# The first pair after a mixture's plain start: x and routing weights by TensorE, or by transposing DMAs and DRAM

## The chip, the cores and the metric

The kernel runs on one core of a Trainium2 chip. TensorE (PE in the profile) multiplies matrices into PSUM; VectorE (DVE), ScalarE (ACT) and GpSimd (POOL) work beside it, and SyncE (SP) issues DMAs, as ScalarE and GpSimd also do. Each engine runs its own list of instructions in order, and an instruction that waits holds all that stand behind it on its engine. The metric is the device time of one execution in microseconds; less is better.

## The reference

For 16 x 512 tokens of 512 features, a softmax over 8 experts gives each token eight routing weights. Every expert is applied to every token, and the results are added with these weights:

```python
probs = softmax(router_logits)                 # 16 x 512 x 8
for e in range(n_experts):                     # 8 experts
    expert_out = np.matmul(x, expert_weights[e])      # 512 x 2048 each
    output += probs[:, :, e:e+1] * expert_out
```

With the eight experts laid side by side this is one product. The left operand z has 8,192 rows of 8 x 512 numbers, x times the routing weight of each expert; the right operand is the 4,096 x 2,048 matrix of all weights.

## The kernel before, in words

**Products.** The product is cut by Strassen's method in Winograd's form, which takes seven products of halves in place of eight. The outer cut makes seven products P1 to P7 of (pairs of) blocks of 256 tokens, four experts and 1,024 columns. Sixteen pairs of token blocks are numbered q. Within one of the outer products the inner cut does the same with 128 tokens, two experts and 512 columns: seven *steps*, in the order 1, 5, 6, 2, 7, 3, 4 (`STEPS`), each of eight matmuls of 512 columns. A *stage* is two such products worked off in turn, step by step, and stages are run one after the other by `run`.

**Third cut.** In most stages steps 1 and 5 of both products are cut a third time (`by_thirds`, class `Thirds`): 14 small products of four matmuls of 256 columns stand in place of four steps of eight matmuls of 512. This needs four more operands from VectorE (operands 5, 6, 3 and 7, made from the z of both products) and small evictions: `ps<-pt,z` and `ps<-ps,z` of 256 columns on VectorE, copies on ScalarE. Before, this is done for stages 1 to 6 of the first outer product and not for stage 0.

**Left operands.** A `Left` holds the z of one product for two experts at a time (`make(0)`, `make(1)`), each one multiplication of a transposed x tile (xT, features by tokens) by a tile pT of routing weights that are the same on all 128 partitions. `queue_s2` makes the operand of step 6 (d), `queue_i` that of steps 7 and 3 (the row `z<-z,d`). The right operands of steps 5, 6, 7 and 4 are differences of the weight blocks (`inner_sums`, rows `w<-w`).

**Order.** VectorE's work waits in a queue of tasks written out by hand. `slack` takes tasks from it while a planned VectorE time (`clock["dve"]`) stays behind a planned TensorE time (`clock["pe"]`); `need` forces a task, with all ahead of it, when a step wants it. From `ordered[0] = True` on, program order is kept on each engine. In the start-up code before that, the framework's scheduler may set the instructions of an engine in another order than the text has.

**The start.** Pairs q = 0 and 1 of P1 are computed without Strassen's method, for two column halves n = 0 and 1, while weights arrive. Their z is made by TensorE: x times a diagonal matrix of routing weights (`early_z0`). GpSimd's queue casts x and weights from f32 to f16 on the way in: two x blocks, three weight blocks of two halves (512 KB in f16 each), then the x of q = 2 and 3 (`cast_x(4)`, `cast_x(6)`), the fourth weight block, and the x of stage 1. `softmax_of_all` computes all routing weights and SP stores them in DRAM (`p_dram`), from which later stages load them, spread over the partitions.

**Stage 0** is q = 2 and 3 of P1. Its xT and pT come from TensorE: `early_xp1`, called for two row blocks each after e = 0 and e = 1 of the plain part's n = 1, transposes x by matmuls with the identity (`ps<-ident,w`) and spreads the weights over the partitions by a matmul of ones with a diagonal (`ps<-h,ones`). VectorE and ScalarE copy the results to SBUF (lines 264 and 262). For that a second small softmax (`early_p(1)`) and four diagonals (`diag_j`) are made on VectorE from logits that SP loads on their own (`load_lg0(1)`).

The last four results of the plain part are copied by ScalarE (line 357) and stored by SP (`kept`).

Of the kernel before, what the change touches and what calls it, by code (L numbers as in the profile page):

```python
# [31 lines left out]
def kernel(  # L32
# [79 lines left out]
    def tt(o, a, b, op):  # L112
        dve(nc.vector.tensor_tensor(out=o, in0=a, in1=b, op=op))  # L113
# [9 lines left out]
    def sp(o, i):  # L123
        note(nc.sync.dma_start(out=o, in_=i))
# [94 lines left out]

    def load_lg0(t):  # L220
        rows = lg_f.rearrange("(q h) e -> q h e", h=2 * HQ)[ds(2 * t, 2), 0:HQ]
        tile_ = lg0[t].rearrange("p (q j) e -> p q j e", j=2)
        if t == 0:
            sp(tile_, rows.rearrange("q (p j) e -> p q j e", p=P))
        else:
            for q in range(2):
                sp(tile_[:, q], rows[q].rearrange("(j p) e -> p j e", p=P))
    lg0 = [cpool.tile([P, 4, E], f32, name=f"lg0_{t}") for t in range(2)]
    load_lg0(0)
    cast_x(0)  # L230
# [6 lines left out]
    with behind():  # L237
        for kn in BLOCKS[:3]:
            cast_block(11, kn, b11[kn], 2 if kn == (0, 0) else 1)
    cast_x(4)  # L240
    cast_x(6)
    cast_block(11, BLOCKS[3], b11[BLOCKS[3]])

    def early_p(t):
        if t == 0:
            return softmax(lg0[t], 4, cpool.tile([P, HE, 4], f16, name="ph0"))
        pf = softmax(lg0[t], 4, cpool.tile([P, HE, 4], f32, name="pf0"))
        odd = pf.rearrange("p e (q j) -> p e q j", j=2)[:, :, :, 1]
        tt(odd[:, 0:2], odd[:, 0:2], odd[:, 2:4], ADD)
        ph = cpool.tile([P, HE, 4], f16, name="ph1")  # L250
        dve(nc.vector.tensor_copy(ph, pf))
        return ph

# [11 lines left out]

    z0 = [zpool.tile([P, HE, C, P], f16, name="z", tag="z") for j in range(4)]
    ph0 = [early_p(0)]

    def diag_e(e):
        return diag(ph0[0][:, e].unsqueeze(2))  # L270

# [6 lines left out]

    ones = cpool.tile([P, P], f16, name="ones")
    nc.vector.memset(ones, 1.0)  # L280
    xp1 = [[xpool.tile([P, C, HQ], f16, name=name, tag="x") for name in ("xT", "pT")] for t in range(2)]

    def diag_j(j):
        return diag(ph0[1][:, :, ds(j % 4, 1)])

    def early_xp1(j, d):
        t, rows = j // 2 - 2, ds(j % 2 * P, P)
        ps = (bank, bank2)[j % 2]()
        for c in range(C):
            mm(ps[:, ds(c * P, P)], xs0[:, j, ds(c * P, P)], ident, c == 0, c == C - 1)  # L290
        evacuate(xp1[t][0][:, :, rows], ps.rearrange("p (c t) -> p c t", c=C), 0)
        ps = (bank, bank2)[j % 2]()
        mm(ps, ones, d.rearrange("p e t -> p (e t)"), True, True)
        evacuate(xp1[t][1][:, :, rows], ps.rearrange("p (e t) -> p e t", e=HE), 1)

# [6 lines left out]
    def load_logits():  # L302
        dve(nc.vector.memset(lg_all[:, 0, 0:1], 0.0))
        dve(nc.vector.memset(lg0[1][:, 0, 0:1], 0.0))
        load_lg0(1)
        for r in range(R):
            sp(lg_all[ds(r * NHQ, NHQ)], lg_v[r])

    def softmax_of_all():
# [11 lines left out]
        for r in range(R):  # L321
            sp(p_dram[:, :, ds(r * J, J)], ph[ds(r * NHQ, NHQ)])

    kept = [dram.tile([2, HQ, NB], f32, name=f"kept_{i}") for i in range(NI)]

# [5 lines left out]
    for n in range(2):  # L331
        ps = [bank2() if n == 0 and j < 2 else bank() for j in range(4)]
        for e in range(HE):
            if n == 0 and e < 2:
                early_z0(e + 2, ds_[e + 2])
                if e == 0:
                    ds_.append(diag_e(3))
            if n == 0 and e == 2:
                ph0.append(early_p(1))
                ds_ = [diag_j(j) for j in range(4, 8)]  # L340
                softmax_of_all()
                w, sums = inner_sums(b11, new_w())
                third = {1: third_sums(w[1])}
# [4 lines left out]
            if n == 1:  # L348
                for j in ((4, 5), (6, 7), (), ())[e]:
                    early_xp1(j, ds_[j - 4])  # L350
                if e == 0:
                    sums[5]()
                elif e == 1:
                    third[5] = third_sums(w[5])
        for j in range(4):
            o = half()
            act(nc.scalar.copy(o, ps[j]))
            sp(kept[j // 2][n].rearrange("(p j) m -> j p m", j=2)[j % 2], o)

    ordered[0] = True  # L360
# [4 lines left out]
    queue = deque()  # L365
    clock = {"pe": 0.0, "dve": 0.0}

# [433 lines left out]
    right = {r: Right() for r in (2, 5, 6, 7, 4, 3)}  # L801
    right[1] = Right(w, {p: Task(2.29, sums[p]) for p in (6, 7, 4)})
    lefts, xs, ps_, bases = {}, {}, {}, {}
# [779 lines left out]

    for stage in range(1, ND):
        thirds[stage] = Thirds(*(p.left for p in stages[stage]), third)
# [55 lines left out]
```

## Time and profile before

| what | us |
|---|---|
| median of 3 runs | 1351.97 (1351.48 to 1352.87) |
| the profiled execution | 1351.78 |
| its span, first to last instruction | 1350.1 |
| TensorE matmuls busy | 1344.0 |
| VectorE busy | 1166.9 |
| ScalarE busy | 281.9 |
| GpSimd busy | 403.9 |

The profiled execution is 1.7 us longer than its span and 0.2 us under the median. In the timeline a row has a start, a length, the engine, the line, the operation and `out<-in` with the program's names, `xN` for N instructions in a row, and in brackets the idle time before it and what ended it. DMA rows give the issuing queue, the size and the microseconds from issue to landing; rows of q0 and q1 give packets, MB and the packets' time as a share of the 16 engines' (it may exceed 100% where packets overlap). q0 carries GpSimd's casts, q1 SP's DMAs.

### The profile page before, as it was taken

Reading aid. Unit: us, or ns where it says so; the run is one execution under the profiler, and the core shown is the slowest. Engines: PE = TensorE matmul, PEld = TensorE weight load, DVE = VectorE, ACT = ScalarE, POOL = GpSimd, SP = SyncE. Lnnn points to the kernel's source line nnn. Section 1 sums busy time; section 2 is a strip of 40 time slices with the busy share of each in tenths; the row PEclk is TensorE's granted clock in tenths of the full one; section 3 lists DMA queues with packets and bytes.
Section 4 is the critical chain, followed back from the end, with each engine's and each line's share of the span. In section 5 each row is a group of like instructions: output and inputs, shape, how many; then the busy total and the mean of one; then the engine's idle time right before and its main releaser. Section 6 shows DMA issues by size and latency. Waiting matters only on the chain.

```text
span 1350.1 us, 19508 instructions
## 1 busy us (share of the span) xinstructions
PE 1344.0 (100%) x7122; PEld 694.3 (51%) x7122; DVE 1166.9 (86%) x1483; ACT 281.9 (21%) x593; POOL 403.9 (30%) x619
## 2 busy tenths in 40 slices
PE   9999999999999999999999999999999999999998
PEld 4465655565544444444444444554555455556564
DVE  7878898989989889797897889889898989898984
ACT  3342423223211111111111100110111111224331
POOL 3123322333323232323312112424334231232342
PEclk9999999999999999999999999999999999999999
DMA  9999989989899999999998889999999989999997
GB/s 181 242 222 240 239 264 242 291 284 290 247 329 282 323 288 286 295 306 265 318 325 265 295 313 189 243 239 216 244 249 226 219 219 310 308 178 230 262 163 132
DMA packets 185392, 346.26 MB, mean 256 GB/s; under 512 B 52176, under 2 KB 81616, under 8 KB 181200
## 3 DMA queue, kind: packets, MB, share of 16 engines
q0 software_dynamic: 84960, 176.72, 58.0%
q1 hardware_dynamic: 97024, 146.15, 35.4%
q10 hardware_dynamic: 3312, 22.15, 4.6%
q8 instruction: 55, 0.90, 0.3%
q14 instruction: 41, 0.34, 0.1%
HBM read 203.19 MB, written 174.26 MB: 280 GB/s over the span
## 4 chain that ended last, share of the span: by engine, by line
PE 98%; DMA 1%; POOL 0%; issue 0%; ACT 0%; POOLq 0%
PE ps L136 77%; PE pt L136 21%; DMA w<-in_expert_weights_dram 1%; POOL w L127 0%; ACT h L1578 0%; POOL ident L234 0%; POOLq L234 0%; POOLq L1625 0%
## 5 line engine op out<-in xcount | busy, mean ns | idle before, releaser
L136 PE MATMUL ps<-w,z 128*128 128x512 f16 (+1 forms) x3884 | 840.0, 372 | 0.0
L136 PEld LDWEIGHTS <-z 128*128 128x128 f16 x5236 | 512.3, 98 | 538.1 <-issue 1.1
L127 POOL DMA_DIRECT2D out_dram<-h x380 | 251.8, 679 | 723.9 <-ACT h L751 321.9
L113 DVE TENSOR_TENSOR h<-ps,h 128x512 f32<-128x512 f32 x318 | 214.9, 686 | 59.1 <-PE ps L136 58.0
L136 PE MATMUL pt<-w,z 128*128 128x512 f16 (+1 forms) x1304 | 253.2, 338 | 0.7 <-DMA w<-in_expert_weights_dram 0.7
L113 DVE TENSOR_TENSOR z<-xT,pT 128x2048 f16<-128x2048 f16 x188 | 226.8, 1217 | 2.2 <-DMA xT<-xs 2.2
L136 PE MATMUL ps<-w,d 128*128 128x512 f16 x880 | 200.7, 379 | 0.0
L738 ACT COPY h<-ps 128x512 f32<-128x512 f32 x102 | 59.8, 586 | 394.0 <-PE ps L136 394.0
L136 PEld LDWEIGHTS <-d 128*128 128x128 f16 x880 | 86.1, 98 | 96.3
L113 DVE TENSOR_TENSOR z<-z,d 128x2048 f16<-128x2048 f16 x110 | 131.8, 1217 | 0.0
L113 DVE TENSOR_TENSOR w<-w 128x1024 f16<-128x1024 f16 (+2 forms) x106 | 116.1, 1114 | 2.6 <-PE ps L136 1.0
L113 DVE TENSOR_TENSOR d<-z 128x1024 f16<-128x1024 f16 x110 | 74.1, 685 | 1.0
L113 DVE TENSOR_TENSOR h<-pt,h 128x512 f32<-128x512 f32 x75 | 51.3, 687 | 27.0 <-PE pt L136 23.9
L751 ACT COPY h<-ps 128x512 f32<-128x512 f32 x54 | 31.6, 586 | 203.5 <-PE ps L136 203.5
L113 DVE TENSOR_TENSOR ps<-ps,h 128x256 f32<-128x256 f32 (+1 forms) x84 | 50.6, 603 | 21.0 <-PE ps L136 15.1
L734 ACT COPY h<-ps 128x512 f32<-128x512 f32 x89 | 49.9, 599 | 70.1 <-PE ps L136 61.3
L127 POOL DMA_DIRECT2D kept<-h x56 | 30.6, 547 | 86.2 <-DVE h L113 48.7
L113 DVE TENSOR_TENSOR z<-z 128x2048 f16<-128x2048 f16 (+1 forms) x52 | 50.5, 978 | 1.5
L730 ACT COPY ps<-ps 128x512 f32<-128x512 f32 x47 | 26.8, 570 | 107.4 <-PE ps L136 59.5
L113 DVE TENSOR_TENSOR h<-h 128x512 f32<-128x512 f32 (+2 forms) x69 | 45.0, 675 | 0.1
L127 POOL DMA_DIRECT2D out_dram<-kept x40 | 42.0, 1150 | 0.2 <-issue 0.2
L136 PEld LDWEIGHTS <-h 128*128 128x128 f16 x384 | 37.6, 98 | 4.3
(109 smaller groups left out, 691.7 us busy)
## 6 DMA issues: line engine op xcount, KB each, us to landing
out_dram<-h POOLq DMA_DIRECT2D x380, 256.0 KB, 7.5
z<-z SPq DMA_DIRECT2D x56, 512.0 KB, 8.7
pT<-p_dram SPq DMA_DIRECT2D x93, 256.0 KB, 8.1
h<-kept SPq DMA_DIRECT2D x88, 256.0 KB, 7.2
w<-wd ACTq DMA_DIRECT2D x20, 1024.0 KB, 8.6
w<-in_expert_weights_dram POOLq DMA_DIRECT2D x33, 512.0 KB, 12.2
xT<-x SPq DMA_DIRECT2D x63, 256.0 KB, 7.8
h<-out_dram SPq DMA_DIRECT2D x60, 256.0 KB, 8.9
```

Of the source, the lines that this page charges most:

```text
L113: dve(nc.vector.tensor_tensor(out=o, in0=a, in1=b, op=op))
L127: note(nc.gpsimd.dma_start(out=o, in_=i, **how))
L136: note(nc.tensor.matmul(ps, z, w, start=start, stop=stop, skip_group_check=True))
L730: act(nc.scalar.copy(self.banks["b"], x))
L734: act(nc.scalar.copy(o[tn], q if p == 5 else x))
L738: act(nc.scalar.copy(o[TN[p]], b if p == 2 else x))
L751: act(nc.scalar.copy(o[tn], b))
```

## The change

Stage 0 takes xT from four transposing DMAs out of the SBUF tile that holds x (`second_x`, on SP) and pT from `p_dram` (`second_p`, on ScalarE's queue, after the copies of n = 0). The TensorE transposes and broadcasts, the second small softmax, its logits and its diagonals are gone. Stage 0's steps 1 and 5 are cut a third time. So that x is there earlier, its two casts move ahead of the second half of the third weight block. Two weight sums (5 and 6) are made in halves, the stage's tasks are queued in another order, and VectorE's planned time starts 7.5 us ahead of TensorE's.

```diff
     with behind():
-        for kn in BLOCKS[:3]:
+        for kn in BLOCKS[:2]:
             cast_block(11, kn, b11[kn], 2 if kn == (0, 0) else 1)
+        cast_w(11, BLOCKS[2], 0, b11[BLOCKS[2]][:, ds(0, C), :])
     cast_x(4)
     cast_x(6)
+    cast_w(11, BLOCKS[2], 1, b11[BLOCKS[2]][:, ds(C, C), :])
     cast_block(11, BLOCKS[3], b11[BLOCKS[3]])
...
-    def early_xp1(j, d):
-        t, rows = j // 2 - 2, ds(j % 2 * P, P)
-        ps = (bank, bank2)[j % 2]()
-        for c in range(C):
-            mm(ps[:, ds(c * P, P)], xs0[:, j, ds(c * P, P)], ident, c == 0, c == C - 1)
-        evacuate(xp1[t][0][:, :, rows], ps.rearrange("p (c t) -> p c t", c=C), 0)
-        ps = (bank, bank2)[j % 2]()
-        mm(ps, ones, d.rearrange("p e t -> p (e t)"), True, True)
-        evacuate(xp1[t][1][:, :, rows], ps.rearrange("p (e t) -> p e t", e=HE), 1)
...
+    def second_p():
+        for t, (_, p) in enumerate(xp1):
+            act(nc.scalar.dma_start(out=p, in_=p_dram[2 * t + 4, ds(P1, HE), :].partition_broadcast(P)))
+
+    def second_x():
+        for j in range(4):
+            note(nc.sync.dma_start_transpose(out=xp1[j // 2][0][:, :, ds(j % 2 * P, P)], in_=xs0[:, j + 4, :]))
...
                 if e == 0:
                     ds_.append(diag_e(3))
+                else:
+                    softmax_of_all()
+                    second_x()
             if n == 0 and e == 2:
-                ph0.append(early_p(1))
-                ds_ = [diag_j(j) for j in range(4, 8)]
-                softmax_of_all()
                 w, sums = inner_sums(b11, new_w())
                 third = {1: third_sums(w[1])}
...
             if n == 1:
-                for j in ((4, 5), (6, 7), (), ())[e]:
-                    early_xp1(j, ds_[j - 4])
                 if e == 0:
-                    sums[5]()
+                    sums[5](ds(0, C))
+                    sums[5](ds(C, C))
...
+        if n == 0:
+            second_p()
...
-    clock = {"pe": 0.0, "dve": 0.0}
+    clock = {"pe": 0.0, "dve": -7.5}
...
-    right[1] = Right(w, {p: Task(2.29, sums[p]) for p in (6, 7, 4)})
+    right[1] = Right(w, {p: Task(2.29, sums[p]) for p in (7, 4)})
+    right[1].task[6] = Task(1.22, lambda: sums[6](ds(C, C)))
...
-    for stage in range(1, ND):
+    for stage in range(ND):
         thirds[stage] = Thirds(*(p.left for p in stages[stage]), third)
...
-    for p in (2, 3):
-        lefts[1, p].queue_make(0)
-    queue.append(need_first[0])
-    for p in (2, 3):
-        lefts[1, p].queue_s2()
-    for p in (2, 3):
-        lefts[1, p].queue_make(1)
+    later(1.22, lambda: sums[6](ds(0, C)))
+    thirds[0].queue()
+    queue.insert(7, need_first[0])
     queue.extend(need_first[1:])
```

As the scheduler builds it, SP's list at the start is: one load of logits, four loads of logits for the softmax of all, the four transposes, the four stores to `p_dram`, the four `kept` stores of n = 0, those of n = 1. ScalarE's is: the copies of z, the softmax of all, the four copies of n = 0, the two loads of pT, the four copies of n = 1.

More of the change, by code (lines that the diff above doesn't have):

```diff
@@ L218, in cast_x @@
         pool(xs0[:, ds(j, 2), :], x_f[ds(j * HQ, HQ), :].rearrange(ROWS[j // 4], p=P))
[L220 to L229, printed above, removed]
+    lg0 = cpool.tile([P, 4, E], f32, name="lg0")
+    sp(lg0.rearrange("p (q j) e -> p q j e", j=2),
+       lg_f.rearrange("(q h) e -> q h e", h=2 * HQ)[ds(0, 2), 0:HQ].rearrange("q (p j) e -> p q j e", p=P))
     cast_x(0)
@@ L237 @@
     with behind():
-        for kn in BLOCKS[:3]:
+        for kn in BLOCKS[:2]:
             cast_block(11, kn, b11[kn], 2 if kn == (0, 0) else 1)
+        cast_w(11, BLOCKS[2], 0, b11[BLOCKS[2]][:, ds(0, C), :])
     cast_x(4)
     cast_x(6)
+    cast_w(11, BLOCKS[2], 1, b11[BLOCKS[2]][:, ds(C, C), :])
     cast_block(11, BLOCKS[3], b11[BLOCKS[3]])
[L244 to L252, printed above, removed]
     def diag(p):
@@ L266 @@
     z0 = [zpool.tile([P, HE, C, P], f16, name="z", tag="z") for j in range(4)]
-    ph0 = [early_p(0)]
+    ph0 = softmax(lg0, 4, cpool.tile([P, HE, 4], f16, name="ph0"))
     def diag_e(e):
-        return diag(ph0[0][:, e].unsqueeze(2))
+        return diag(ph0[:, e].unsqueeze(2))
     def early_z0(e, d):
@@ L277, in early_z0 @@
             evacuate(z0[j][:, e], ps.rearrange("p (c t) -> p c t", c=C), j)
-    ones = cpool.tile([P, P], f16, name="ones")
-    nc.vector.memset(ones, 1.0)
     xp1 = [[xpool.tile([P, C, HQ], f16, name=name, tag="x") for name in ("xT", "pT")] for t in range(2)]
-    def diag_j(j):
-        return diag(ph0[1][:, :, ds(j % 4, 1)])
-    def early_xp1(j, d):
-        t, rows = j // 2 - 2, ds(j % 2 * P, P)
-        ps = (bank, bank2)[j % 2]()
-        for c in range(C):
-            mm(ps[:, ds(c * P, P)], xs0[:, j, ds(c * P, P)], ident, c == 0, c == C - 1)
-        evacuate(xp1[t][0][:, :, rows], ps.rearrange("p (c t) -> p c t", c=C), 0)
-        ps = (bank, bank2)[j % 2]()
-        mm(ps, ones, d.rearrange("p e t -> p (e t)"), True, True)
-        evacuate(xp1[t][1][:, :, rows], ps.rearrange("p (e t) -> p e t", e=HE), 1)
     R = 4
@@ L303, in load_logits @@
         dve(nc.vector.memset(lg_all[:, 0, 0:1], 0.0))
-        dve(nc.vector.memset(lg0[1][:, 0, 0:1], 0.0))
-        load_lg0(1)
         for r in range(R):
```

## The prediction

> **What bounds the kernel now.** First the page's busy shares, then TensorE's waits (us in total, times, longest), then TensorE's timeline.
>
> ```profile
> PE 1344.0 (100%) x7122; PEld 694.3 (51%) x7122; DVE 1166.9 (86%) x1483; ACT 281.9 (21%) x593; POOL 403.9 (30%) x619
> ...
> PE every L95 <- DVE h L92: 1.3, 1, 1.3
> PE pt L136 <- DMA w<-in_expert_weights_dram: 0.7, 2, 0.4
> PE ps L136 <- DVE lg L304: 0.3, 1, 0.3
> ```
>
> TensorE waits 2.3 us in the whole run, all before the place of the change. So TensorE work taken away is worth its full length, and so costs any new wait. The time is made by where TensorE's stream stands. That stream around the change (start, length; a row's last 0.38 us is the drain):
>
> ```profile
> 24.73 4.05 PE L136 MATMUL ps<-w,z 128*128 128x512 f16 x18
> 28.62 0.39 PE L136 MATMUL ps<-ident,w 128*128 128x128 f16 x4
> ...
> 29.49 3.62 PE L136 MATMUL ps<-w,z 128*128 128x512 f16 x16
> 32.95 0.39 PE L136 MATMUL ps<-ident,w 128*128 128x128 f16 x4
> ...
> 33.83 10.52 PE L136 MATMUL ps<-w,z 128*128 128x512 f16 x48
> 44.19 3.62 PE L136 MATMUL pt<-w,z 128*128 128x512 f16 x16
> 47.64 3.62 PE L136 MATMUL ps<-w,d 128*128 128x512 f16 x16
> ...
> 58.00 3.62 PE L136 MATMUL pt<-w,z 128*128 128x512 f16 x16
> ...
> 64.91 1.04 PE L136 MATMUL pt<-w,z 128*128 128x256 f16 x8
> 71.02 2.32 PE L136 MATMUL ps<-w,d 128*128 128x512 f16 x10
> ```
>
> A step of both products takes 3.45 us (44.19 to 47.64). Two steps before 47.64, at 40.7, stage 0 begins; step 7 ends at 58.0, and stage 1 begins at 64.91.
>
> **What the change removes on TensorE.** The transposes and broadcasts of the pair stand from 28.62 to 29.49 and from 32.95 to 33.83: 0.87 + 0.88 = 1.75 us. Stage 0's steps 1 and 5 take 6.91 us as 32 matmuls of 512 columns. Split a third time they are 56 of 256 columns, as in stage 1, where they last from 64.91 to 71.02: 6.11 us, 0.80 less. Together -2.55 us if nothing waits, with TensorE at stage 0 by 40.7 - 1.75 = 39.0.
>
> **What it removes elsewhere.** VectorE loses the second small softmax, four diagonals and four casts; ScalarE four casts; SP two loads of logits. TensorE waited for none of these, so they are worth nothing themselves. Removed VectorE work does let the softmax of all start when its logits are there, some 3 us before 19.28; that gain is lost on SP, next.
>
> **What it moves: SP's order.** In the text the stores of the routing weights to DRAM (p_dram) come ahead of the transposes, but as built SP has the four transposes first, and an instruction that waits holds all behind it. They wait for x, whose casts stand one 512 KB weight half earlier on POOL:
>
> ```profile
> 8.06 0.79 POOL L127 DMA_DIRECT2D w<-in_x_dram  x1
> w<-in_x_dram POOLq DMA_DIRECT2D x1, 256.0 KB, 18.7
> 10.21 0.72 POOL L127 DMA_DIRECT2D w<-in_x_dram  x1 [1.36 <-DMA w<-in_expert_weights_dram]
> w<-in_x_dram POOLq DMA_DIRECT2D x1, 256.0 KB, 17.9
> 20.71 0.71 POOL L127 DMA_DIRECT2D xs<-in_x_dram  x1 [1.51 <-DMA w<-in_expert_weights_dram]
> xs<-in_x_dram POOLq DMA_DIRECT2D x1, 256.0 KB, 15.7
> 25.68 2.67 SPq L124 DMA_DIRECT2D p_dram<-h  x4
> p_dram<-h SPq DMA_DIRECT2D x1, 48.0 KB, 8.9
> 55.50 5.71 SPq L432 DMA_TRANSPOSE xT<-xs  x4
> ```
>
> x lands at 26.8 and 28.1 now, 1.3 us per 256 KB; 2.6 us earlier it lands at 24.2 and 25.5. Four transposes hold SP 5.7 us: 24.2 to 29.9. The stores then go out from 29.9 to 32.6, 4.2 us later than now (25.68), though their data wait earlier. The weight half moved behind x lands at 25.5 + 2.6 = 28.1; TensorE wants it at 28.6, so it costs nothing, by 0.5 us.
>
> **Where the routing weights arrive.** The last of today's stores starts at 27.7 and lands 8.9 us later, at 36.6, just after the casts end (20.71 + 15.7 = 36.4). The reason is in the queues (q0 casts, q1 SP):
>
> ```profile
> q0 software_dynamic: 626, 0.62, 124.4%
> ...
> q0 software_dynamic: 388, 0.38, 112.1%
> q1 hardware_dynamic: 389, 0.05, 30.8%
> ...
> q0 software_dynamic: 144, 0.14, 96.3%
> q1 hardware_dynamic: 135, 0.05, 30.9%
> ...
> q1 hardware_dynamic: 731, 0.18, 133.4%
> ```
>
> The windows are 26 to 29, 30 to 32, 49 to 50 and 51 to 52 us. In the first the casts run alone, 209 packets per us, and SP's stores, issued from 25.68, have not begun: some 4 us from issue to first packet. In the second both queues move one packet each, 194 per us. In the third (transposes beside a cast) 135 and 144. In the fourth the transposes are all but alone: 731 per us, 0.18 MB, 250 bytes each. Four transposes of 128 KB are then some 2,050 packets, the four stores (192 KB in pieces of 128 bytes) 1,536.
>
> So the transposes' packets flow from 24.2 + 4 = 28.2. At that time the casts have 8.2 us x 209 = 1,710 packets left; at 194 per us they end at 37.0, and 1,710 packets of the transposes have gone too. Left on q1 are 340 of these and the 1,536 of the stores, 1,876 at 731 per us: 2.5 us, so the stores land at 39.5. Only then can ScalarE issue the two loads of the weights (broadcast):
>
> ```profile
> pT<-p_dram SPq DMA_DIRECT2D x1, 256.0 KB, 4.2
> pT<-p_dram SPq DMA_DIRECT2D x1, 256.0 KB, 3.8
> pT<-p_dram SPq DMA_DIRECT2D x1, 256.0 KB, 5.2
> ```
>
> I take 4.2, the middle: 43.7, and z 1.2 us later at 44.9. Bounds: from below, the transposes cost nothing and the stores land at 36.6 as now, the load takes 3.8, z is there at 41.6. From above, both queues run at the third window's rates: casts end at 40.1, the stores land at 42.8, load 5.2, z at 49.2. ScalarE's four copies of the last plain block queue behind the load's wait; they need 2.05 us from about 40.7, end at 42.8, before stage 0 can begin anyway, so nothing.
>
> **What VectorE must do after that.** All of stage 0's VectorE work now stands behind the late z:
>
> ```profile
> 37.10 2.35 DVE L113 TENSOR_TENSOR z<-xT,pT 128x2048 f16<-128x2048 f16 x2
> ...
> 41.58 1.29 DVE L113 TENSOR_TENSOR d<-z 128x1024 f16<-128x1024 f16 x2
> ...
> 45.05 4.49 DVE L113 TENSOR_TENSOR w<-w 128x4096 f16<-128x4096 f16 x2
> 49.45 2.36 DVE L113 TENSOR_TENSOR z<-z,d 128x2048 f16<-128x2048 f16 x2
> ...
> 56.52 0.69 DVE L113 TENSOR_TENSOR h<-z 128x1024 f16<-128x1024 f16 x1
> 57.25 0.69 DVE L113 TENSOR_TENSOR h<-h,z 128x1024 f16<-128x1024 f16 x1
> ...
> L113 DVE TENSOR_TENSOR ps<-pt,z 128x256 f32<-128x256 f32 x8 | 3.5, 433 | 10.9 <-PE pt L136 9.1 <-ACT z L967 1.7
> ```
>
> Counted from the end of the first z, in the built order: second z 1.2; four operands of the third split to 3.9 (0.73 where one needs the last); half a weight sum to 5.0; two d to 6.2; four evictions of 0.43, the last waiting for TensorE, to 8.5; the z of the other experts to 10.8; two weight sums to 15.2; the two z-d to 16.4 and 17.5. TensorE beside it: the third split, held by z, the operands and the evictions, ends at about 8.5 instead of 6.1; steps 6 and 2 at 15.4; step 7 needs z-d and starts at 16.4, ends at 16.4 + 3.45 = 19.9. Now it ends at 58.0; with z at 44.9 it ends at 64.8: +6.8 us, in which the -2.55 is contained. Behind that, VectorE makes stage 1's operands, with four evictions between, in some 9 us from 17.5, and stage 1 begins at 26.8: just in time, so nothing more; from there its 86% wins the lead back. So 1351.78 (the profiled execution; the median is 0.2 higher) + 6.8 = 1358.6. Bounds: z at 41.6 gives 61.5, +3.5, 1355.3; z at 49.2 gives 69.1, +11.1, 1362.9.
>
> **A rule that speaks against the change.** TensorE would stand idle from 39.0 to 44.9.
>
> ```profile
> 1.30 4.45 PE L95 MATMUL every<-h 128*128 128x512 f16 x10 [1.30 <-DVE h L92]
> ```
>
> The first ten matmuls took 0.445 us each, those at 24.73 (4.05 - 0.38)/17 = 0.216: this TensorE starts at half rate. The Trainium skill (TensorE: Matmul & The Clock Gate, "What's actually happening") says that an idle window of about 3.4 us brings half rate back until it has been busy for as long; no row of this trace has such a pause.
>
> **Rivals.**
> 1. *Half rate after the pause.* If it lasts over the third split alone, VectorE's chain hides all but 0.3 us. If it lasts over step 6 too, that takes 6.9 us, step 2 ends at 8.8 + 6.9 + 3.45 = 19.2 and step 7 at 22.6: 2.7 more, 1361.3. For it: the pause. Against: the work after it is dense.
> 2. *No change: SP's packets are not held behind the casts.* With 3.8 us from issue to landing, stores at 31.9 + 3.8 = 35.7, load 39.5, z 40.7, step 7 ends at 60.6: +2.6, 1354.4. It decides if the stores land before 35.7. Against: 8.9 us in today's row under the same casts. The Trainium skill (DMA: Bandwidth & Descriptors, "Anatomy of one DMA") gives 2.0 us plus bytes at 436 GB/s for GpSimd's DMAs; by that estimate z comes at 37.9 and the time is 1351.8.
> 3. *Faster: all is hidden.* 1351.8 - 2.55 = 1349.2. The load must have landed by about 34, so the stores by 30, when SP only begins to issue them. It could come only if SP issued them ahead of the transposes.
>
> **How the numbers follow.** A change within 0.2% (2.7 us) cannot be told from none here. Late weights 0.76, half rate on top 0.09, rival 2 0.09, rival 3 0.03; 0.03 for a further loss not seen (casts slowed so that TensorE waits for weights). Slower 0.88, same 0.09, faster 0.03. The range 1354.3 to 1363.0 takes the two bounds and the edge of rival 2.
>
> **What would show it.** Right: SP's first transpose at about 24 and first store near 30; stores landing at 39 to 40; VectorE's first z of the pair waiting for the pT load until about 43.7; TensorE idle near 6 us before stage 0, its step 7 waiting for z-d; step 3 starting near 65. Wrong if the stores land before 36, if step 7 does not wait for VectorE, or if a matmul after the pause takes 0.43 us for long.

## The result and the profile after

The changed kernel takes 1358.92 us (median of 6 runs, 1358.21 to 1361.58), the kernel before 1351.71 beside it: a ratio of 1.0057, 95% interval 1.0044 to 1.007. It is slower by 7.2 us; 1358.6 had been forecast. The profiled execution took 1358.42 us with a span of 1356.7, 6.6 longer than before.

The page's busy shares of the changed kernel, and below them TensorE's waits (us in total, times, longest):

```profile
PE 1343.2 (99%) x7126; PEld 695.4 (51%) x7126; DVE 1164.4 (86%) x1476; ACT 282.3 (21%) x596; POOL 404.7 (30%) x619
```

```profile
PE pt L136 <- DVE z L113: 5.6, 1, 5.6
PE every L95 <- DVE h L92: 1.3, 1, 1.3
PE ps L136 <- DMA w<-in_x_dram: 1.0, 2, 0.6
PE ps L136 <- DVE z L113: 1.0, 1, 1.0
```

TensorE has less to do than before, and waits for z in one piece of 5.6 us and in one of 1.0. Both are new. The 1.0 us for x is new too, but it lies in the first 7 us, and the plain part begins at 9.98, as before (9.97). TensorE's timeline of the changed kernel shows where they stand:

```profile
24.76 14.41 PE L136 MATMUL ps<-w,z 128*128 128x512 f16 x66
44.78 1.89 PE L136 MATMUL pt<-w,z 128*128 128x256 f16 x8 [5.61 <-DVE z L113]
...
53.25 3.62 PE L136 MATMUL ps<-w,d 128*128 128x512 f16 x16
56.70 3.62 PE L136 MATMUL ps<-w,z 128*128 128x512 f16 x16
61.30 10.53 PE L136 MATMUL ps<-w,z 128*128 128x512 f16 x48 [0.98 <-DVE z L113]
71.67 1.04 PE L136 MATMUL pt<-w,z 128*128 128x256 f16 x8
```

The plain part stands where it stood (24.76 against 24.73). It now runs in one row to 39.17, with nothing of the pair in between. Then comes the pause, the third split from 44.78 to 53.25, steps 6 and 2, a second wait, and step 7 from 61.30. Stage 1 begins at 71.67 and not at 64.91: 6.76 later, and that is the whole loss, since the span grew by 6.6.

The parts of the 6.76 can be read off these rows. Gone are 2.55 us of TensorE work. Come are the 5.61 of idle time; 0.98 ahead of step 7; the drain ahead of each of the two waits, 0.17 us (a row's end, 3.62, less the 3.45 to the next row's start where nothing waits); and the third split, which takes 8.47 us and not 6.11, 2.36 more. 5.61 + 0.98 + 0.34 + 2.36 - 2.55 = 6.74.

Why z was late is in the lists of SP and ScalarE (timelines of the changed kernel, one fence each), and in how long their DMAs took from issue to landing:

```profile
23.44 7.96 SPq L298 DMA_TRANSPOSE xT<-w  x4
31.51 4.76 SPq L124 DMA_DIRECT2D p_dram<-h  x4
```

```profile
39.07 0.93 ACTq L294 DMA_DIRECT2D pT<-p_dram  x2
```

```profile
p_dram<-h SPq DMA_DIRECT2D x1, 48.0 KB, 6.7
...
p_dram<-h SPq DMA_DIRECT2D x1, 48.0 KB, 4.6
...
pT<-p_dram ACTq DMA_DIRECT2D x1, 256.0 KB, 4.4
...
pT<-p_dram ACTq DMA_DIRECT2D x1, 256.0 KB, 4.8
```

The four transposes hold SP from 23.44 to 31.4. Only then do the stores go out, the first at 31.51 and the last near 34.3; it lands 4.6 us later, at 39.0. At 39.07 ScalarE issues the loads, and 4.4 us later, at 43.5, the first is there. VectorE's timeline shows z waiting for just that:

```profile
43.49 2.36 DVE L113 TENSOR_TENSOR z<-xT,pT 128x2048 f16<-128x2048 f16 x2 [11.34 <-DMA pT<-p_dram]
...
48.69 1.22 DVE L113 TENSOR_TENSOR w<-w 128x2048 f16<-128x2048 f16 x1
49.83 1.28 DVE L113 TENSOR_TENSOR d<-z 128x1024 f16<-128x1024 f16 x2
...
53.35 2.35 DVE L113 TENSOR_TENSOR z<-xT,pT 128x2048 f16<-128x2048 f16 x2
55.62 4.49 DVE L113 TENSOR_TENSOR w<-w 128x4096 f16<-128x4096 f16 x2
60.02 2.35 DVE L113 TENSOR_TENSOR z<-z,d 128x2048 f16<-128x2048 f16 x2
```

Before, the same first z began at 37.10. From 43.49 on VectorE works through its list with hardly a gap, and step 7 begins at 61.30, just after the first z-d.

The queues in windows of the changed kernel (q0 the casts, q1 SP): 28 to 34, and the one from 37 to 38 us.

```profile
q0 software_dynamic: 956, 0.94, 92.0%
q1 hardware_dynamic: 951, 0.24, 29.9%
...
q1 hardware_dynamic: 1499, 0.20, 139.0%
```

Over six us both queues move nearly the same number of packets, 159 per us each, however small those of q1 are (0.24 MB in 951). That is what the Trainium skill (DMA: Bandwidth & Descriptors, "Queues, rings and completion order") states: each DMA engine takes turns between its queues packet by packet. From 37 on the casts are through, and 1,499 packets of some 130 bytes pass in one us, nearly as many as the stores' 1,536 pieces.

The granted clock (column PEclk, after the busy times of PE, PEld, DVE, ACT and POOL), in windows of 3.41 us of the changed kernel:

```profile
38.57:41.98 3.41, 0.60 (x3) 0.10 (x1) 0.00 (x0) 1.94 (x4) 0.00 (x0) 1.00 1.05 343
41.98:45.39 3.41, 0.61 (x3) 0.43 (x4) 1.90 (x2) 0.12 (x1) 0.00 (x0) 0.50 0.97 342
45.39:48.81 3.42, 3.42 (x17) 2.05 (x16) 3.18 (x6) 1.33 (x4) 0.00 (x0) 0.50 1.07 321
48.81:52.22 3.41, 3.25 (x30) 2.77 (x29) 3.30 (x6) 0.89 (x4) 0.00 (x0) 1.00 1.35 147
```

So after the pause TensorE did run at half rate, for 4 us of work from 44.78 to 48.81. That is the first half of the prediction's rival 1, and what it costs was the first open question.

### The profile page after: what moved, and what is told of

It is laid out like the page before. It is cut to its first block, busy times and chain, and to the rows that moved or that the text cites. A ratio compares the mean times of both kernels' runs of the same rounds, so it can differ in the third digit from the quotient of the medians.

```text
span 1356.7 us, 19512 instructions
## 1 busy us (share of the span) xinstructions
PE 1343.2 (99%) x7126; PEld 695.4 (51%) x7126; DVE 1164.4 (86%) x1476; ACT 282.3 (21%) x596; POOL 404.7 (30%) x619
## 4 chain that ended last, share of the span: by engine, by line
PE 95%; DVE 0%; ACT 0%; issue 0%
PE ps L136 75%; PE pt L136 20%; DVE z L113 0%; ACT h L1556 0%
## 5 line engine op out<-in xcount | busy, mean ns | idle before, releaser
L136 PE MATMUL pt<-w,z 128*128 128x512 f16 (+1 forms) x1288 | 249.1, 337 | 6.5 <-DVE z L113 5.6
L707 ACT COPY ps<-ps 128x512 f32<-128x512 f32 x47 | 26.8, 570 | 108.8 <-PE ps L136 69.5
L136 PEld LDWEIGHTS <-h 128*128 128x128 f16 x416 | 41.1, 99 | 5.7 <-DVE h L113 0.7
```

The source lines that it names most:

```text
L136: note(nc.tensor.matmul(ps, z, w, start=start, stop=stop, skip_group_check=True))
L707: act(nc.scalar.copy(self.banks["b"], x))
```

## The experiments

The theory: the stores, held on SP by the transposes and slowed by the casts, make pT and z late; behind z, VectorE's list sets the end, and half rate is hidden in it. The rivals: half rate itself costs time; the transposes cost time of their own; the third split costs time rather than saving 0.80. A fourth question was whether a part of the change is a gain. The runs are numbered e1 to e12, and the expectations name them so.

### Stores ahead of the transposes (e1)

Of the changed kernel, with program order kept for both on SP:

```diff
-            sp(p_dram[:, :, ds(r * J, J)], ph[ds(r * NHQ, NHQ)])
+            dve(nc.sync.dma_start(out=p_dram[:, :, ds(r * J, J)], in_=ph[ds(r * NHQ, NHQ)]))
...
-            note(nc.sync.dma_start_transpose(...))
+            dve(nc.sync.dma_start_transpose(...))
```

> The changed kernel with SP's order at the start turned round: the four stores of the routing weights go out ahead of the four transposes. Theory (the routing weights are late because SP and its packets serve the transposes first): the stores go out near 22 and land near 34 (4 us to the first packet, 1,536 packets at 194 per us beside the casts), the transposes now stand behind them and land near 39, so the first z comes at about 41 in place of 44.7, step 7 ends 19.9 us later at about 61, and the time is about 1354.5 (0.2% over the kernel before). Rival (SP's order does not matter, the casts alone hold the stores up): the stores land at 36 to 39 and the time stays within 1 us of 1358.9.

Measured: 1356.53 us (1355.71 to 1361.84), ratio 1.0041 (1.0027 to 1.0054). That is 2.4 under the changed kernel and 2 above what was expected. SP issues the stores 9.6 us earlier, from 21.90, but they land only 3.1 us earlier, at 35.9, as their packets still take turns with the casts' (445 beside 442 in the 2.3 us from 28.7). The loads go out at 35.88; the first z begins at 40.78, the second, whose load lands last, at 42.80. TensorE's timeline:

```profile
42.06 1.05 PE L136 MATMUL pt<-w,z 128*128 128x256 f16 x8 [2.97 <-DVE z L113]
...
44.81 1.04 PE L136 MATMUL ps<-w,h 128*128 128x256 f16 x4 [1.70 <-DVE h L113]
...
61.01 10.53 PE L136 MATMUL ps<-w,z 128*128 128x512 f16 x48 [0.98 <-DVE z L113]
```

The clock falls here too, from 43.95 to 50.77, later against the work than in the changed kernel, so that TensorE has 6.0 us of work at half rate and not 4.0. VectorE's timeline shows two evictions of the third split waiting for the slow TensorE:

```profile
50.22 0.43 DVE L113 TENSOR_TENSOR ps<-pt,z 128x256 f32<-128x256 f32 x1 [0.94 <-PE pt L136]
51.04 0.43 DVE L113 TENSOR_TENSOR ps<-pt,z 128x256 f32<-128x256 f32 x1 [0.39 <-PE pt L136]
```

Here the half rate is not hidden, and step 7 begins only 0.3 us earlier. This execution was also the slowest of the six (1361.84): behind stage 1, between 190 and 700 us, it loses 3.7 us against the changed kernel's, which says nothing of the change. So where the median's 2.4 us come from can't be read from its trace. The record has one sign: the three runs with a mean granted clock of 0.998 or 0.999 took 1355.7 to 1356.2 us, the three with 0.997, like this one, 1356.9 to 1361.8. That a shorter drop of the clock makes the difference is not shown. What follows: SP's order is a part of the loss, but turning it round does not bring back even half.

### No full pause (e2)

Of the changed kernel, between the plain part and stage 0; nothing reads the result:

```diff
+    warm = bank2()
+    for i in range(20):
+        mm(warm, z0[0][:, 0, 0], b11[0, 0][:, 0, :], True, True)
     ordered[0] = True
```

> The changed kernel with 20 matmuls that nothing reads put on TensorE between the plain start and stage 0, 4.3 us of the 5.6 us in which it waits for z. They keep TensorE's clock up and take no engine from anybody. Theory (VectorE's list behind the late z sets when step 7 begins, so the half clock after the pause is hidden): no more than 0.5 us less than the changed kernel, 1358.4 to 1358.9, with the granted clock at 1.00 from 44 to 48 us. Rival (the half clock after the pause is a cost of its own): 2 to 3 us less, about 1356.5.

Measured: 1359.36 us (1358.23 to 1366.38), ratio 1.0064 (1.0042 to 1.0085): no gain. TensorE's timeline, and the granted clock in two windows of 3.41 us:

```profile
38.19 4.48 PE L136 MATMUL pt<-w,z 128*128 128x512 f16 x20
...
61.23 10.53 PE L136 MATMUL ps<-w,z 128*128 128x512 f16 x48 [0.98 <-DVE z L113]
```

```profile
41.36:44.77 3.41, 1.38 (x8) 0.46 (x6) 1.35 (x2) 1.16 (x3) 0.00 (x0) 1.00 0.87 290
44.77:48.18 3.41, 3.41 (x16) 2.00 (x17) 3.17 (x5) 1.09 (x3) 0.00 (x0) 0.50 0.83 251
```

The pause is 2.03 us in place of 5.61, and step 7 still begins at 61.23. So the pause as such costs nothing; what stands behind z on VectorE does. The expectation that the clock stays at 1.00 was a miss in this execution: it fell although TensorE had worked for 1.4 of the 3.41 us before. TensorE's work at half rate lasted 3.4 us and not 4.0, too small a difference to show much. But two of the five runs have a mean granted clock of 1.00, where a single window at half rate makes 0.999 or less (3.41 us of 1,357 at half), so in these the clock did not fall. They took 1358.39 and 1359.36 us: without the half rate the kernel is no faster. In the changed kernel it is hidden.

### One part alone: x by DMA, weights by TensorE (e3)

Of the changed kernel; early_p, load_lg0, ones and diag_j are back, softmax_of_all stands where it stood before the change, and of early_xp1 the half for the weights is back:

```diff
+    def early_p1(j, d):
+        t, rows = j // 2 - 2, ds(j % 2 * P, P)
+        ps = (bank, bank2)[j % 2]()
+        mm(ps, ones, d.rearrange("p e t -> p (e t)"), True, True)
+        evacuate(xp1[t][1][:, :, rows], ps.rearrange("p (e t) -> p e t", e=HE), 1)
...
-        if n == 0:
-            second_p()
```

> The changed kernel with the routing weights of the pair made by TensorE again (second small softmax, diagonals, matmuls of ones, 0.86 us of TensorE), x still by transposing DMAs, third split of stage 0 kept. Theory (the store and the load of the routing weights are what is late): z waits for the transposes alone, which landed at 35.0 and 37.9, so second z near 39.2; TensorE does not stop before stage 0 (39.9), VectorE's list lets step 7 end at about 57.8 against 58.0 before: 1350.5 to 1352.0, no change against the kernel before that can be told. Rival (the transposes are as late as the weights): a wait of several us before stage 0 stays and the time is 1354 or more.

Measured: 1352.50 us (1352.16 to 1353.66), ratio 1.0006 (0.9996 to 1.0015). With the weights made on the core, 6.3 of the 7.2 us are gone (0.9 are left against the kernel before beside it, 1351.56). The stores are as late as in the changed kernel (issued from 31.73), and nothing waits for them. z starts at 37.48, TensorE's waits at stage 0 are 0.27, 0.64 and 0.98 us, the clock stays at 1.00. The 0.98 stands at the same place as in the changed kernel (VectorE's first z, then TensorE):

```profile
37.48 2.47 DVE L113 TENSOR_TENSOR z<-xT,pT 128x2048 f16<-128x2048 f16 x2 [4.04 <-issue]
```

```profile
55.33 10.53 PE L136 MATMUL ps<-w,z 128*128 128x512 f16 x48 [0.98 <-DVE z L113]
```

Step 7 ends at 55.33 + 3.45 = 58.78. The prediction's list for VectorE, 19.9 us from the end of the first z (here 38.7), gives 58.6: it holds in another kernel, with z 6 us earlier and full clock. Step 7 begins 16.6 us behind the end of the first z here, at full clock, and 16.6 us behind it in the changed kernel, with 4 us at half rate (61.30 - 44.7): this shows a second time that the half rate took nothing there. What the change saves on x, about half of the 1.75 us of TensorE work, and the 0.80 of the third split are lost in these three waits.

### The other part alone: weights through DRAM, x by TensorE (e4)

Of the changed kernel:

```diff
+    def early_x1(j):
+        ps = (bank, bank2)[j % 2]()
+        for c in range(C):
+            mm(ps[:, ds(c * P, P)], xs0[:, j, ds(c * P, P)], ident, c == 0, c == C - 1)
+        evacuate(xp1[j // 2 - 2][0][:, :, ds(j % 2 * P, P)], ps.rearrange("p (c t) -> p c t", c=C), 0)
...
-                    second_x()
```

> The changed kernel with x of the pair transposed by TensorE again (0.89 us of TensorE), the routing weights still through DRAM, third split of stage 0 kept; no transposing DMA at the start. Theory: the stores go out near 22, land near 34 as nothing but the casts stands beside them, the loads land near 39, first z at 40.2, step 7 ends near 60.1: 1353.8, so more than half of the loss is gone but not all. Rival (the transposes have no part in it): the stores land with the end of the casts at 36.5 or later, first z at 42 or later, 1355.5 or more.

Measured: 1354.46 us (1354.30 to 1355.54), ratio 1.0021 (1.0012 to 1.0031). SP's timeline, TensorE's, and the median of the four stores from issue to landing:

```profile
21.99 2.67 SPq L124 DMA_DIRECT2D p_dram<-h  x4
```

```profile
57.15 10.53 PE L136 MATMUL ps<-w,z 128*128 128x512 f16 x48 [0.98 <-DVE z L113]
```

```profile
p_dram<-h SPq DMA_DIRECT2D x4, 48.0 KB, 8.8
```

Without transposes SP issues the stores at 21.99, 3.7 us earlier than before the change: that is the gain by the earlier softmax, which in the changed kernel the transposes take away. They still need 8.8 us beside the casts; the last lands at 34.7, the loads at 39.0 and 40.5, and TensorE waits at stage 0 for 1.17, 0.85 and 0.98 us. So with weights by way of DRAM the kernel is 2.9 us slower even without transposes. This and the last run both hold the third split, which has a price of its own (next), so 0.9 and 2.9 are not the prices of the two parts, and can't be added up. But neither comes near 7.2: most of the loss needs both, and what they do to each other is their meeting on SP and in its queue (stores issued at 31.51 with the transposes, at 21.99 without).

### The third split: taken out of the changed kernel (e8), and put into the one before (e6)

Of the changed kernel; stage 0's tasks are queued as in the kernel before:

```diff
-    for stage in range(ND):
+    for stage in range(1, ND):
         thirds[stage] = Thirds(*(p.left for p in stages[stage]), third)
```

> The changed kernel without the third split of stage 0: x by transposing DMAs and weights from DRAM as late as there, steps 1 and 5 whole, VectorE without the four operands and the four small evictions (some 4.5 us less behind the late z). By TensorE's columns alone the time rises by 0.80, to 1359.7. By VectorE's list the wait before step 7 goes and TensorE is the bound from the late z on: step 7 begins 44.7 + 13.8 = 58.5, plus what the half clock then costs (half of the 4 us between 44.7 and 48.8 at 0.5, so 2.0): 60.5 in place of 61.3, and the time is 1358.1; without a cost of the clock it would be 1356.1.

Measured: 1358.01 us (1357.20 to 1359.62), ratio 1.0048 (1.0032 to 1.0063). The first two rows of stage 0 in TensorE's timeline:

```profile
44.84 5.51 PE L136 MATMUL ps<-w,z 128*128 128x512 f16 x16 [5.91 <-DVE z L113]
50.19 3.62 PE L136 MATMUL pt<-w,z 128*128 128x512 f16 x16
```

The first sixteen matmuls take 5.35 us to the next row's start, where a step at full rate takes 3.45. Here the half rate is on the path: TensorE's own columns set the pace, and the half rate costs 1.9 us. Even so this kernel is not slower than the split one, which has 0.8 us less TensorE work.

Of the kernel before:

```diff
-    for stage in range(1, ND):
+    for stage in range(ND):
         thirds[stage] = Thirds(*(p.left for p in stages[stage]), third)
...
+    thirds[0].queue()
+    queue.insert(6, need_first[0])
     queue.extend(need_first[1:])
```

> The kernel before with one part of the change alone: steps 1 and 5 of stage 0 cut a third time, x and routing weights still by TensorE. By TensorE's columns alone the time falls by the 0.80 us of the forecast, to 1350.9. By VectorE's list (from the first z at 38.3 it takes 19.9 us to the point where step 7 can be through, plus the whole of sum 6 in place of half of it, 1.1 us) step 7 ends at about 58.9 in place of 58.0, and the time is 1352.4.

Measured: 1353.74 us (1352.98 to 1354.93), ratio 1.0016 (1.0007 to 1.0024): slower by 2.1. TensorE's timeline:

```profile
55.83 10.53 PE L136 MATMUL ps<-w,z 128*128 128x512 f16 x48 [1.58 <-DVE z L113]
```

Step 7 now waits for VectorE and begins 1.3 us later than before, although stage 0 began 0.3 earlier in this execution (40.44 against 40.74). The third split was to take 0.80 us from TensorE, and puts four operands and four evictions on VectorE, which is the one that sets this stage. With VectorE's tasks in this order it is a loss by itself, larger than the expectation by VectorE's list (0.8).

### The weight sums ahead of z (e5)

Of the changed kernel:

```diff
     later(1.22, lambda: sums[6](ds(0, C)))
+    queue.extend(need_first)
     thirds[0].queue()
-    queue.insert(7, need_first[0])
-    queue.extend(need_first[1:])
```

> The changed kernel with three weight sums (the second half of 6, then 7 and 4: 1.2 + 4.5 us) put ahead of the two z on VectorE, into the 11.3 us in which it waits for the routing weights; nothing else moves. Theory (VectorE's list behind the late z sets when step 7 begins): TensorE's wait of 0.98 us ahead of step 7 goes, step 7 begins near 60.2 in place of 61.3, and the time is 1.1 us less, 1357.8. Rival (that wait belongs to something else, the weights or the banks): step 7 begins at 61.3 still and the time is 1358.9.

Measured: 1358.46 us (1357.37 to 1359.27), ratio 1.0049 (1.0035 to 1.0063). While z waits for its load, VectorE makes the sums that need only weights. The wait ahead of step 7 is gone; the row runs on from step 2:

```profile
57.04 13.98 PE L136 MATMUL ps<-w,z 128*128 128x512 f16 x64
```

Step 7 begins at 57.04 + 3.45 = 60.49, 0.8 us earlier, although z came 0.3 later than in the changed kernel (43.83). That the list behind z sets step 7 is shown by this; but 5.7 us of VectorE work moved away gained only 0.8, since from there TensorE, late and at half rate, sets the end. The median is 0.5 lower than that of the changed kernel, within the intervals of both.

### The parts that might gain, together (e7, and e11 the same again)

Of e3:

```diff
+            if stage == 0 and n == 6:
+                flush(left.b.task["s2"])
-            slack(0.4375, LAG if n < 6 else 1.3)
+            slack(0.4375, (LAG if n < 6 else 1.3) if stage else 3.0)
...
+    queue.extend(need_first[:2])
     thirds[0].queue()
-    queue.insert(7, need_first[0])
-    queue.extend(need_first[1:])
+    queue.extend(need_first[2:])
```

> Routing weights by TensorE, x by transposing DMAs, third split of stage 0, and VectorE's list put right: the second half of sum 6 and sum 7 ahead of the two z, both d ahead of the evictions, the other z behind them. If the lateness of the weights and VectorE's list are all that stood against the change, no wait of over 0.3 us is left at stage 0, step 7 ends near 56.5 (58.0 before) and the time is about 1350.3, under the kernel before by 0.1%. If the transposing DMAs cost something further (the third split held by x, casts slowed), it stays at 1351.5 or more.

Measured: 1350.83 us (1350.20 to 1351.93), ratio 0.9993 (0.9984 to 1.0002). Two sums ahead of z and both d ahead of the evictions leave 0.23 us of waiting at stage 0, and stage 1 begins 1.55 us earlier than before the change (rows of the plain part, of stage 0 from its start, and of stage 1):

```profile
24.25 4.05 PE L136 MATMUL ps<-w,z 128*128 128x512 f16 x18
...
39.36 1.04 PE L136 MATMUL pt<-w,z 128*128 128x256 f16 x8
...
46.09 3.62 PE L136 MATMUL ps<-w,d 128*128 128x512 f16 x16
...
63.36 1.04 PE L136 MATMUL pt<-w,z 128*128 128x256 f16 x8
```

Of the 1.55 us, 0.48 are there when the first of these rows begins (24.25 against 24.73), before any of the removed work; this start differs from run to run. From that row to stage 0 it takes 15.11 us and not 16.01: the 0.90 of x's transposes. The third split takes 6.73 us in place of 6.91, so even with VectorE's list put right 0.18 of its forecast 0.80 come through.

> e7 once more, beside the runs of e9 and e10: 1350.8 again (0.8 under the kernel before). If that difference was chance, 1351.6.

The same kernel again: median 1350.81 of 11 runs (1350.30 to 1358.99), ratio 1.0006 (0.9992 to 1.0019). The median repeats, 0.8 under the kernel before, but the runs scatter more, and the interval reaches further past 1. The scatter goes with the clock: eight runs with a mean granted clock of 1.00 took 1350.30 to 1351.65 us, the three with 0.999, 0.998 and 0.997 took 1355.03, 1356.92 and 1358.99. Why it fell in these is not known. So the best version found is as fast as the kernel before, or 0.8 us faster: the runs don't prove a gain.

### Weights through DRAM, but early (e9, e12, e10)

Of e7; the weights of the pair come from the second small softmax and go through p_early, a DRAM tile of 4 KB. SP keeps program order for its store and for the transposes, and second_p is called after the copies of n = 0, as in the changed kernel:

```diff
+    def rows_of_p(ph):
+        ps = bank()
+        mm(ps[0:4 * HE, 0:P], ph.rearrange("p q e j -> p (q e j)"), ident, True, True)
+        dve(nc.vector.tensor_copy(p_rows, ps[0:4 * HE, 0:P]))
+        dve(nc.sync.dma_start(out=p_early.rearrange("q e (j p) -> (q e j) p", p=P), in_=p_rows))
+
+    def second_p():
+        for t, (_, p) in enumerate(xp1):
+            act(nc.scalar.dma_start(out=p, in_=p_early[t].partition_broadcast(P)))
...
                 else:
+                    rows_of_p(ph0[1])
                     second_x()
```

> From e7: the pair's routing weights still come from the second small softmax, but go through DRAM like the others: one TensorE transpose of 128 columns makes them rows, one store of 4 KB on SP's list ahead of the transposing DMAs takes them to a small DRAM tile, and ScalarE loads them spread over the partitions. The eight broadcasts by TensorE (1.75 us with x in the kernel before; some 0.9 of it the weights' part), their diagonals and evictions are gone. If what made the change slow is only that the weights pass through DRAM behind the transposes and the casts, this costs nothing: the store goes out by about 21 us and lands by 30, the loads by 35, ahead of x (last transpose near 38), z at 37.5 as in e3, no half clock, and with 0.9 us of TensorE less than e7 (1350.8): 1349.6 to 1350.3. If any store to DRAM and load back in this stretch comes too late, pT lands after 39 and z is the last again: 1353 to 1355.

Measured: 1357.66 us (1356.37 to 1358.08), ratio 1.0041 (1.0028 to 1.0053): nearly as slow as the changed kernel, though the store lands at 20.1. ScalarE's timeline, and landings of the small store and of the third transpose (issued at 26.12):

```profile
37.50 1.01 ACTq L295 DMA_DIRECT2D pT<-p_early  x2
```

```profile
p_early<-p_rows SPq DMA_DIRECT2D x1, 4.0 KB, 4.4
...
xT<-w SPq DMA_TRANSPOSE x1, 11.4
```

ScalarE was through with its copies by 27, and the loads' data were in DRAM for 17 us. The first load goes out at 37.50; the third transpose lands at 26.12 + 11.4 = 37.5. As built, the load waits for that transpose as well as for its data: the two use the same semaphore, a counter that announces the landing of a DMA. The trace gives each of these instructions with its semaphore. The DMAs of SP and ScalarE use eight in turn; the third transpose and the first load both have number 112, the first store to p_dram and the second load 115, and each load is issued only when the earlier DMA on its number has landed (37.48 and 38.16). The result is the pause of the changed kernel, from another cause: a wait that no data ask for. In the changed kernel itself the first load shares number 108 with the fourth transpose; but that lands at 37.93 and the last store, whose data the load needs, at 38.97, so there the data set it.

Of e9; the stores to p_dram are split off from `softmax_of_all`, and second_p is called here and no longer after the copies of n = 0:

```diff
-                    second_x()
+                    p_all = softmax_of_all()
+                    second_p()
+                    second_x()
+                    store_all(p_all)
```

> e9 with the two loads of the pair's weights given out ahead of the transposes, so that neither of them shares a completion semaphore with a transpose or a store to p_dram. In e9 the 4 KB store landed at 20.08 us, but its two loads went out at 37.50 and 38.18, each just after the landing of an earlier DMA on the semaphore that it was to use (the third transpose at 37.48, the first store to p_dram at 38.16). If that held them, they now go out at about 21 us and land by 30 beside the casts, the transposes are the last to land (near 38, as in e3), z starts near 37.5, no half clock, TensorE waits under 0.7 us at stage 0: 1350.0 to 1351.0. If weights by way of DRAM are late here whatever holds them, z starts after 40 again and the time stays above 1354. If the loads' 512 KB push the casts back by over 2 us, x or a weight half is late instead: 1351.5 to 1353.

Measured: 1352.42 us (1351.74 to 1353.32), ratio 1.0006 (0.9997 to 1.0015). ScalarE's timeline:

```profile
21.39 0.34 ACTq L295 DMA_DIRECT2D pT<-p_early  x1
21.76 0.45 ACTq L295 DMA_DIRECT2D pT<-p_early  x1
```

The loads now go out at 21.4 and 21.8 and land by 28.2. They now have numbers 108 and 110, on which nothing of the transposes or the stores stands ahead of them. That shows what held them, and that weights by way of DRAM need not be late here. But it is the third case of the expectation. In the 6 us from 22 on the casts' queue moved 945 packets beside the loads, where it moved 1,223 in e9 (rows of q0 with packets, MB and their share; e9 first, e12 second):

```profile
q0 software_dynamic: 1223, 1.21, 121.4%
```

```profile
q0 software_dynamic: 945, 0.93, 92.8%
```

All later casts land 2.0 us later (the last at 39.26 in place of 37.24), with them the last weight sum, and z, which VectorE makes behind it, starts at 39.28. TensorE waits for 0.73, 0.81 and 0.19 us at stage 0.

> e9 with the x of the pair cast ahead of the whole third weight block and not only ahead of its second half, 1.3 us earlier. If x's transposes set z in e9, z comes 1.3 us earlier and what TensorE still waits at stage 0 (0.2 to 0.9 us) goes, against a wait for the weight half that lands 2.6 us later than in e9 (in the changed kernel it landed some 2.6 us ahead of its use: 0 to 0.5 us): 1349.2 to 1350.3. If the weight half is late, TensorE waits at about 24.7 us for 1 us or more: 1350.5 to 1351.5.

This one is e9 with x cast one weight half earlier: 1357.75 us (1356.09 to 1358.42), ratio 1.0042 (1.0028 to 1.0056). Its second load is held to 38.62, by the landing of a store to p_dram, and nothing is gained; the question it was made for, whether the earlier x is worth anything, stays open.

## Why the prediction was right, point by point

- **TensorE's own gain, 2.55 us, at stage 0 by 39.0.** It was done with the plain part at 39.17, drain included. Right.
- **SP's order, and how long the transposes hold SP.** The order was as built. The term was mis-sized: four transposes took 7.96 us of SP and not 5.7. The row used for it (55.50) stood beside fewer casts (220 packets of casts in 5.7 us, 1,465 in 8.0 in the changed kernel); that this is the reason is likely, not shown. They began at 23.44 and not 24.2, so the stores went out from 31.5 and not 29.9, 1.6 us later than the forecast.
- **Packets.** Beside the casts 159 per us and queue, not 194: the 194 came from the stores' small pieces, and the row with transposes beside a cast (135 and 144) was kept for the upper bound alone. Alone 1,499 and not 731, since the stores' pieces of 128 bytes pass faster than the transposes' packets, from which 731 was taken. Two terms wrong in opposite directions: the last store landed at 39.0, forecast 39.5. The landing was right partly because errors cancelled. That the casts' end sets it was right: the last stores go through in the us after the casts have ended.
- **The load, 4.2, and z at 44.9.** 4.4 us, and the end of the first z at 44.7. Right, with the luck of the landing in it.
- **VectorE's list behind z.** The third split ends 8.5 us after z by the forecast: 53.25 - 44.7 = 8.55. Step 7 begins 16.4 after z: 61.30 - 44.7 = 16.6. Stage 1 begins 26.8 after: 71.67 - 44.7 = 27.0. Three numbers within 0.2 us, and the list held again with z at 38.7. The sum, +6.8, is +6.76 at stage 1 and +6.6 in the span; the medians differ by 7.2.
- **The half rate.** By the row of the start (0.445 us each) the prediction held half rate after the pause possible, and it came: 0.50 for two windows of 3.41 us. The rule that it quoted from the Trainium skill (TensorE: Matmul & The Clock Gate, "What's actually happening"), half rate after an idle window of some 3.4 us, fits only roughly: the window ahead of the drop held 0.60 us of work. It ended at 48.81, inside the third split, which lasted to 53.25. That VectorE's chain hides it if it lasts over the third split alone was right: the runs of e2 at full clock were no faster, and e3 has the same 16.6 us from z to step 7. In e8, without the split, the same drop cost 1.9 us, and in e1, where it came later against the work, evictions waited for TensorE. So rival 1 was near: the cover is the split's VectorE work, and only when the drop falls early in it.
- **Rival 2, no queueing.** Against it, the stores took 4.6 to 6.7 us in the changed kernel, 8.8 where they went out early beside the casts, and landed at 39.0, not before 35.7. The estimate that the prediction made from the Trainium skill (DMA: Bandwidth & Descriptors, "Anatomy of one DMA"), which gives its figures for GpSimd's DMAs, is 2.1 us for 48 KB: two to four times too short for SP's stores under a full queue. (By the prediction's own list z at 37.9 gives 1351.6, not the 1351.8 that it states.)
- **Rival 3, the gain of 2.55.** The prediction took the split's 0.80 us as a gain that the late z hides. The run that puts it into the kernel before shows that, with VectorE's tasks in that order, it is no gain even without a late z: +2.1 us; with the list put right (e7) it takes 0.18 us less than the two whole steps. This is the one point at which the reasoning, not a size, was short: the TensorE column was believed although VectorE's list was worked out two parts further on.
- **The moved weight half, nothing.** It landed at 27.2, wanted at 28.6: no wait in TensorE's row of 66 matmuls. Right.

What stays open: why turning SP's order round gains 2.4 us in the median but 0.3 us at step 7 in its profiled execution, what the transposes and the weights by DRAM each cost without the third split, and whether the version with the sums first is faster than the kernel before.

## What to carry to other kernels

When work moves from an engine that is always busy to a chain of DMAs, the price is the landing of the last link under the queue's load at that moment; read it from rows of the same stretch, count packets per queue, and look up what stands ahead of each link in its issuing engine's list as built. Then work out the list of the engine behind the late operand: here VectorE's list, not TensorE's columns, gave the end to within 0.2 us, and it is also what tells whether a cut such as the third split is worth anything in a stage. A load that starts much later than its data land, at the landing of an unrelated DMA, may be held by a completion semaphore that the two share, as in e9; give it out ahead of the slow ones, and count what its bytes take from the transfers beside it.

## What the runs showed of the hardware that was not expected

- The clock fell after a pause of only 2.03 us, with TensorE busy for 1.4 of the 3.41 us before (e2, in the profiled execution; in two others of its five runs it did not fall), and did not fall where the longest pause was 1.58 us (e6). In the profiles it changes at whole multiples of 3.41 us: in the changed kernel 11 of them after full rate began at 4.44, and 2 more at half rate. The prediction, with the Trainium skill (TensorE: Matmul & The Clock Gate, "What's actually happening"), had thought of a whole idle window.
- How long transposing DMAs hold SP is not fixed: four took 5.71 us at 55 us of the kernel before, 7.96 in the changed kernel, and 10.63 in e1, where four stores went out ahead of them; the first alone took 1.3 us in the changed kernel and 4.2 in e1. This fits a queue that is full of earlier work.
- The share of a queue beside the casts goes by packets: in e12 0.52 MB of ScalarE's loads, 288 packets on a third queue, cost the casts 278 packets of 1,223 in 6 us, and 2.0 us of every later landing.
